# All eight PSUM banks as single ones of one pool, in both MLPs

## The chip, the core and the metric

The kernel runs on one core of a Trainium2 chip. The metric is the device time in microseconds (us) of one execution. Lower is better. The kernel runs three times, and the median is given beside a profile of one execution.

## What is computed

One inference step of a two-layer encoder on 576 frames (512 of a new stream, 64 of a running one) with 1024 features. Layer 0 mixes frames by causal pooling, layer 1 by sparse attention (an indexer scores the keys, the best are kept, softmax runs over these). Each is followed by an MLP with a squared ReLU:

```python
def _mlp(h, w_up, w_down):
    u = jax.nn.relu(h @ w_up)          # (frames, 1024) @ (1024, 4096)
    return (u * u) @ w_down            # (frames, 4096) @ (4096, 1024)

x = x + y                              # y from the pooling mixer or attention
x = x + _mlp(_rmsnorm(x, norm_mlp[i]), mlp_w_up[i], mlp_w_down[i])
```

A last RMS norm ends the step. The outputs are `y` for both streams, the new pooling states and the new keys, values and indexer keys.

## The kernel before

Everything stays on the core: `x`, the residual, is in SBUF as eight blocks of 128 features by 576 frames, and the weights stream through it. A float32 product is made of three matmuls: each operand is split into a high part (rounded to fp32r, a form that the matmul takes) and a low part that holds what was left. ACT makes the high part of a weight block (`wh`, L181), DVE the low part (`wl`, L182). Each matmul has a 128 x 128 weight and 288 frames (`HT`, half of 576), so one of its outputs fills 288 of the 512 float32 columns that a PSUM bank has.

PSUM has eight banks. A `stage` opens pools for a part of the program; `ps` is a pool of pairs (a tile of two neighbouring banks, taken with `psum`), `po` a pool of single banks (`psum1`). In the stages of both MLPs there are two pairs (banks 0 to 3) and four singles (4 to 7). Tiles of a pool are taken in the order in which its buffers come free.

An MLP has four chunks of 1024 hidden features. Chunk 0's Up part is a plain product: eight tiles (i = 0 to 7), each 48 matmuls by `project` (L305) into a tile `up` of two halves. `finished` then calls `activated`, which takes ReLU times the norm's factor (`rbm`, L460 or L462: one DVE instruction if the tile is a pair, two if it is a tuple of two singles) and squares it on ACT. All Up tiles are pairs but i = 2, which comes before the norm's factors are known.

All other parts use Strassen's scheme in the form with seven products. One "seven" (the function `seven`) makes a 2 x 2 block from seven products of twelve matmuls each (`product`, L504), in three single banks named `a`, `b` and `c`. Bank `b` takes b11, then t2, t3 and t4 in turn; between them the running sum is read out: after b11 ACT copies it to `a` (L533), and after t2, t3 and t4 the callbacks `b`, `hi1` and `lo1` read it. Bank `a` takes b21, bank `c` takes t1 and b22. So t4 may start only when the reading after t3 is done. The callbacks are in two classes: `Down` updates `x` on DVE (L562), `Up` reads the banks on DVE (L612 for `b` after t3, L618 for `c`, L595 for ReLU) and makes the operands of the Down products (`u`, with lower parts on DVE at L476). Chunks 1 to 3 have four Up sevens each, the last of them called final, and every chunk has four Down sevens, chunk 3 of layer 1 only three, since the last two output blocks are made as plain products at the end of the program (`last`, tiles `dn`). For these, `left_over` (L497) parks the hidden block b12 of each Up seven in PSUM, two to a pair, until the end.

The order of PE, DVE and ACT is made by a scheduler that plays the program forward with costs and sets each engine's instructions by when their operands and buffers come free; only in `last` is it written by hand. So the pools decide what stands between the products of a seven. Each engine then runs its list in order. A semaphore wait holds up all that stands behind it on that engine.

```python
    with stage(more=RAWS[1]):
        with stage(xs=1, slots=1, tmps=6, ps=3, po=2):
            pool_mixer()
        with stage(xs=1, u=1, acts=1, xt=1, sums=4, ps=2, po=4):
            mlp(0, 1, late=KT)
    with stage(under=1, xs=1, queries=1, slots=1, cst2=1, tmps=5), ExitStack() as parts:
        parts.enter_context(stage(ps=2, po=4))
        attention(parts)
    with stage(u=1, xs=1, acts=1, xt=1, sums=4, more=RAWS[1], ps=2, po=4):
        mlp(1, 3, end=last)
```

The attention stage has the same two pairs and four singles before and after. Its first work is the projections `pj` (L305), in pairs.

Of the kernel before, what the change touches and what calls it, by code (L numbers as in the profile page):

```python
# [12 lines left out]
ALU = mybir.AluOpType  # L13
# [3 lines left out]
P = 128  # L17
# [5 lines left out]
HT = T // 2  # L23
# [23 lines left out]
RAWS = (4, 3)  # L47
# [9 lines left out]
def pool_dsa_kernel(ctx: ExitStack, tc: tile.TileContext, a, o):  # L57
    nc = tc.nc
    act, dve, pool, pe = nc.scalar, nc.vector, nc.gpsimd, nc.tensor
# [11 lines left out]
    def uid(s):  # L71
        count[0] += 1
        return f"{s}_{count[0]}"
# [3 lines left out]
    @contextmanager  # L77
    def stage(**pools):


        with ExitStack() as st:
            for name, bufs in pools.items():
                space = {"space": PSUM} if name in ("ps", "po") else {}
                phase[name] = st.enter_context(tc.tile_pool(name=uid(name), bufs=bufs, reuse_waits="tile", **space))
                st.callback(phase.pop, name)
            yield
# [7 lines left out]
    def pair_slot(tag, s, dt=F32R, n=T):  # L94
        return slot(tag, s, dt)[:, :2 * n].rearrange("p (h t) -> p h t", h=2)
# [9 lines left out]
    def psum(s="ps"):  # L105
        return phase["ps"].tile([P, 2, 512], F32, tag="ps", name=uid(s))

    def psum1(s="po"):
        return phase["po"].tile([P, 512], F32, tag="po", name=uid(s))

    def f32(t):
        return t.bitcast(F32)

    def halves(t):
        return t.rearrange("p (h t) -> p h t", h=2)
# [165 lines left out]
    def next_block(sub=dve):  # L281
        return [next_unit(5 - i, sub) for i in range(2)]

    def at(w, k):

        return [t[:, (k % 4) * P:(k % 4 + 1) * P] for t in w[k // 4]]

    def split(dst, src, scale=None, sub=dve):

        if scale is None:  # L290
            act.copy(dst[:, 0], src)
            sub.tensor_tensor(dst[:, 1], src, f32(dst[:, 0]), ALU.subtract)
        else:
            act.activation(dst[:, 0], src, AF.Copy, scale=scale)
            dve.scalar_tensor_tensor(dst[:, 1], src, scale, f32(dst[:, 0]), ALU.mult, ALU.subtract)

    def project(pt, w, xs, between=iter(()), cols=((0, HT), (HT, HT))):

        n = len(xs)
        for k in range(n):  # L300
            next(between, None)
            wh, wl = at(w, k)
            for i, (wt, part) in enumerate(((wh, 0), (wh, 1), (wl, 0))):
                for h, (c, m) in enumerate(cols):
                    pe.matmul(  # L305
                        pt[h][:, :m] if isinstance(pt, tuple) else pt[:, h, :m], wt, xs[k][:, part, c:c + m],
                        start=(k == 0 and i == 0), stop=(k == n - 1 and i == 2),
                    )
# [76 lines left out]
    def split_x(gi, norm, room, late=0):  # L385

        xs = []
        for k in range(KT + late):
            if k < KT:
                t = room(k)  # L390
                split(t, x[k], gv[:, gi, k:k + 1])
                xs.append(t)
            if k >= late:
                norm.add(k - late)
        return xs

    def mlp(layer, gi, late=0, end=None):
# [13 lines left out]
        xs = split_x(gi, norm, lambda k: pair_slot("xs", "xs"), late)  # L411
# [4 lines left out]
        xt = []  # L416
        parked = []
# [74 lines left out]

        def left_over(j, b12):

            if j % 2 == 0:
                parked.append(psum("rest"))
            act.copy(parked[-1][:, j % 2, :HT], b12)  # L497

        def product(bank, w, operand, factor, js, first=False):
            for j in js:  # L500
# [175 lines left out]
        todo, us = [], []  # L676
        for i in range(KT):
            w = next_block()
            pt = (psum1("up"), psum1("up")) if i == 2 else psum("up")
            project(pt, w, xs, spread() if i == 2 else iter(()))  # L680
            todo.append((i, pt, us))
            if i == 1:
                norm.stats()
            if i < 2:
                continue
            for t in todo:
                finished(*t)
            todo.clear()
            if i in (3, 5):
                r = 2 * i - 6  # L690
                x_sums(i // 2 - 1, rough[:, r:r + 3], rough[:, r + 3])
# [17 lines left out]
        for c in range(1, 4):  # L709
            us = []  # L710
            for j in range(half):
                up = Up(c, j)
# [7 lines left out]
        if end:  # L720
            rest = []
            for j in range(half):
                if j % 2 == 0:
                    t = x_sums_tile()
                rest.append(t[:, j % 2])
                split(rest[j], parked[j // 2][:, j % 2, :HT])
            b11, b22, b21 = ([u[:, FACTORS.index(f)] for u in us] for f in ("b11", "b22", "b21"))
            end([rest + b22, b11 + b21])

    def last(parts):  # L730

        norm = Norm("f", lambda: slot("xs", "sq", F32)[:, :T])
        for k in range(KT - LAST):
            norm.add(k)
        ws = [next_block() for _ in range(LAST)]

        def finish(c, n, aside, rest):
            t = slice(c, c + n)
            room = halves(slot("xs", "room", F32))
            st = psum1("st")  # L740
            token_sums(st, norm.s2[:, t], n=n, block=BLOCK, final=False)
            if c:
                awake(KEEP[0])
            token_sums(st, rest, n=n, block=BLOCK, first=False)
            r = rms(st, n, BLOCK)
            if c:
                awake(KEEP[1])
            for k in aside:
                act.activation(x[k][:, t], x[k][:, t], AF.Copy, scale=gv[:, 4, k:k + 1])
            yield  # L750
            diag = diagonals(r, n, room[:, 0], BLOCK)
            banks = [psum1("rb") for _ in range(2 if c else 1)]
            for pb in banks:
                pe.matmul(pb[:, :n], ones[:BLOCK], diag[:BLOCK, :n], start=True, stop=True)
            pb = banks[0]
            rb = room[:, 1, :n]
            act.copy(rb, banks[-1][:, :n])
            yield
            for k in range(KT):
                if k == 4:  # L760
                    yield
                if k in aside:
                    pool.tensor_tensor(x[k][:, t], x[k][:, t], rb, ALU.mult)
                else:
                    dve.scalar_tensor_tensor(x[k][:, t], x[k][:, t], gv[:, 4, k:k + 1], pb[:, :n], ALU.mult, ALU.mult)
                if c and k > 3:
                    (nc.sync if k % 2 else act).dma_start(o["y"][:, k, t], x[k][:, t])
                elif k % 2:
                    nc.sync.dma_start(o["y"][:, k - 1:k + 1, t], x.t[k // 2][:, :, t])

        def awake(n):

            pt = psum("dn")
            for _ in range(n):
                pe.matmul(pt[:, 0, :HT], ws[0][0][0][:, :P], parts[0][0][:, 0], start=True, stop=True)

        def during(steps):

            for k in range(LAST * KT):
                if k in NORM_STEPS:  # L780
                    next(steps)
                yield

        before = between = iter(())
        with tc.manual_schedule(engines={ENG.PE, ENG.DVE, ENG.Activation}):
            for c, n, us in ((0, HT, parts[0]), (HT, HT, parts[1])):
                t = slice(c, c + n)
                s2 = norm.s2[:, t]
                for j in range(LAST):
                    k = KT - LAST + j  # L790
                    pt = psum("dn")
                    project(pt, ws[j], us, between, cols=((0, n),))
                    dve.tensor_tensor(x[k][:, t], x[k][:, t], pt[:, 0, :n], ALU.add)
                    sq = norm.room()[:, :n]
                    act.activation(sq, x[k][:, t], AF.Square)
                    if j < LAST - 1:
                        dve.tensor_tensor(s2, s2, sq, ALU.add)
                for _ in before:
                    pass
                before = finish(c, n, FINAL_ASIDE[c > 0], sq)  # L800
                between = during(before)
            for _ in before:
                pass
# [675 lines left out]
    x = Residual()  # L1479
    with stage(more=RAWS[1]):  # L1480
        with stage(xs=1, slots=1, tmps=6, ps=3, po=2):
            pool_mixer()
        with stage(xs=1, u=1, acts=1, xt=1, sums=4, ps=2, po=4):
            mlp(0, 1, late=KT)
    with stage(under=1, xs=1, queries=1, slots=1, cst2=1, tmps=5), ExitStack() as parts:
        parts.enter_context(stage(ps=2, po=4))
        attention(parts)
    with stage(u=1, xs=1, acts=1, xt=1, sums=4, more=RAWS[1], ps=2, po=4):
        mlp(1, 3, end=last)


# [94 lines left out]
```

## Time and profile before

| | |
|---|---|
| median of 3 runs | 1085.96 us (1085.89 to 1086.33) |
| profiled execution | 1085.9 us, its span 1084.1 us |
| PE (matmul) busy | 1051.9 us, 97% of the span |
| DVE busy | 909.1 us, 84% |
| ACT busy | 627.1 us, 58% |
| POOL busy | 264.6 us, 24% |
| layer 0's MLP | about 41 to 414 us |
| attention | about 414 to 690 us |
| layer 1's MLP and the end | about 690 to 1084 us |

PE is TensorE's matmul queue, PEld its weight loads, DVE the vector engine, ACT the scalar engine, POOL GpSimd. In a row of a timeline stand the start (us), the duration, the engine, the line, the operation, the output and its inputs, and their shapes; several of the same kind in a row are one row with their count, and the bracket names the idle time ahead of it and what ended that. A row of waits gives the total, the times and the longest. In windows each engine has its busy time and a count of instructions; behind POOL stand the granted PE clock, the DMA share and GB/s.

### The profile page before, as it was taken

The page shows a single profiled execution, that of the slowest core. Times are in us where ns is not written, and L with a number is a line of the kernel's source. Part 1 is how long each engine was busy: PE and PEld are TensorE (multiplying, and loading weights), DVE is VectorE, ACT ScalarE, POOL GpSimd, SP SyncE. Part 2 cuts the span into 40 slices and gives each one's busy share as a digit, 9 for nine tenths or more (in the row PEclk, how much of TensorE's full clock was granted, in tenths as well). Part 3 has the DMA queues.
Part 4 walks back from the last instruction along what each step waited for, and adds up shares of the span by engine and source line. Part 5 has one row for each costly group of instructions (what it writes and reads, how often), then busy time and mean ns, then how long its engine had stood idle before and what let it go on. Part 6 is the DMA issues. An engine that isn't in the chain of part 4 may idle for free.

```text
span 1084.1 us, 21647 instructions
## 1 busy us (share of the span) xinstructions
PE 1051.9 (97%) x7942; PEld 1024.0 (94%) x7942; DVE 909.1 (84%) x1845; ACT 627.1 (58%) x1240; POOL 264.6 (24%) x285
## 2 busy tenths in 40 slices
PE   9999999999999999999999999999999999999996
PEld 8999998999999999999988888999999999999895
DVE  7788989879978987869999944688989879979974
ACT  8555466447546654444477776455467447547641
POOL 4100111111111100237686892000111111111001
PEclk9999999999999999999989999999999999999998
DMA  8343676676676654447632454333676666667512
GB/s 252 94 102 89 171 166 151 166 163 169 151 166 165 156 161 165 128 153 191 201 108 68 129 170 123 126 108 97 166 165 157 162 164 165 154 170 161 125 51 88
DMA packets 94459, 157.66 MB, mean 145 GB/s; under 512 B 13729, under 2 KB 25296, under 8 KB 94352
## 3 DMA queue, kind: packets, MB, share of 16 engines
q1 hardware_dynamic: 68720, 109.80, 33.3%
q0 software_dynamic: 15840, 28.84, 17.1%
q10 hardware_dynamic: 9792, 17.63, 5.2%
q8 instruction: 62, 1.02, 0.4%
q14 instruction: 45, 0.37, 0.1%
HBM read 141.15 MB, written 10.89 MB: 140 GB/s over the span
## 4 chain that ended last, share of the span: by engine, by line
PE 78%; DVE 9%; ACT 3%; POOL 3%; issue 3%; DMA 2%; SPq 0%; DVEq 0%; POOLq 0%; ACTq 0%
PE b L504 28%; PE c L504 15%; PE up L305 9%; PE a L504 7%; PE pj L305 7%; PE wo L305 2%; DVE wl L182 2%; PE wa L305 1%; PE pb L1011 1%; PE sc L1284 1%; PE dn L305 1%; PE pt L1310 1%; POOL p L1263 1%; DVE u L476 1%; PE o L1342 1%
## 5 line engine op out<-in xcount | busy, mean ns | idle before, releaser
L181 ACT CAST wh<-raw 128x512 fp32r<-128x512 f32 (+1 forms) x316 | 194.8, 620 | 232.6 <-PE b L504 75.4
L182 DVE TENSOR_TENSOR wl<-raw,wh 128x512 fp32r<-128x512 f32 (+1 forms) x294 | 205.9, 703 | 38.6 <-ACT wh L181 30.2
L504 PE MATMUL b<-u,wh 128*128 128x288 f32 x992 | 203.1, 296 | 2.2 <-ACT a L533 1.7
L504 PEld LDWEIGHTS b<-u,wh 128*128 128x128 f32 x992 | 159.5, 188 | 4.3 <-ACT a L533 3.6
L181 ACT CAST wh<-sum 128x512 fp32r<-128x512 f32 x165 | 101.4, 620 | 80.3 <-PE b L504 36.3
L504 PE MATMUL b<-u,wl 128*128 128x288 f32 x496 | 145.5, 296 | 0.0
L182 DVE TENSOR_TENSOR wl<-sum,wh 128x512 fp32r<-128x512 f32 x165 | 112.0, 687 | 20.6 <-ACT wh L181 18.5
L238 POOL DMA_DIRECT2D sum<-in_w_down x31 | 27.1, 891 | 327.4 <-DVE u L476 86.6
L504 PE MATMUL c<-u,wh 128*128 128x288 f32 x496 | 103.3, 297 | 0.9 <-DVE u L476 0.6
L504 PEld LDWEIGHTS b<-u,wl 128*128 128x128 f32 x496 | 92.8, 188 | 0.0
L305 PE MATMUL up<-xs,wh 128*128 128x288 f32 x512 | 89.6, 296 | 1.0 <-DVE x L1477 0.8
L504 PE MATMUL b<-xt,wh 128*128 128x288 f32 x384 | 77.9, 296 | 8.0 <-DVE v L612 8.0
L476 DVE TENSOR_TENSOR u<-v,u 128x864 fp32r<-128x864 f32 (+2 forms) x100 | 82.1, 825 | 0.9 <-ACT u L473 0.5
L504 PEld LDWEIGHTS c<-u,wh 128*128 128x128 f32 x496 | 80.1, 188 | 2.5 <-DVE x L562 1.5
L473 ACT CAST u<-v 128x864 fp32r<-128x864 f32 (+2 forms) x100 | 72.7, 730 | 8.8 <-DVE v L491 5.4
L504 PE MATMUL b<-xs,wh 128*128 128x288 f32 x384 | 76.8, 295 | 0.0
L305 PEld LDWEIGHTS up<-xs,wh 128*128 128x128 f32 x512 | 74.6, 188 | 2.0 <-ACT wh L181 1.0
L504 PE MATMUL c<-u,wl 128*128 128x288 f32 x248 | 73.2, 295 | 0.0
L238 POOL DMA_DIRECT2D sum<-in_w_up x24 | 20.7, 863 | 209.4 <-DVE wl L182 132.5
L504 PEld LDWEIGHTS b<-xt,wh 128*128 128x128 f32 x384 | 61.3, 188 | 9.6 <-DVE v L612 9.6
L454 ACT ACTIVATE v<-v 128x288 f32<-128x288 f32 (+1 forms) x112 | 52.0, 476 | 16.5 <-DVE v L595 14.1
L305 PE MATMUL pj<-xs,wh 128*128 128x288 f32 x352 | 61.3, 295 | 0.0
(287 smaller groups left out, 2738.4 us busy)
## 6 DMA issues: line engine op xcount, KB each, us to landing
raw<-in_w_up SPq DMA_DIRECT2D x128, 256.0 KB, 3.0
raw<-in_w_down SPq DMA_DIRECT2D x128, 256.0 KB, 2.9
raw<-in_w_o ACTq DMA_DIRECT2D x32, 256.0 KB, 2.8
sum<-in_w_down SPq DMA_DIRECT2D x31, 256.0 KB, 2.9
sum<-in_w_down POOLq DMA_DIRECT2D x31, 256.0 KB, 4.5
raw<-in_w_down POOLq DMA_DIRECT2D x31, 256.0 KB, 5.0
raw<-in_w_in ACTq DMA_DIRECT2D x30, 256.0 KB, 3.0
sum<-in_w_up SPq DMA_DIRECT2D x24, 256.0 KB, 3.0
```

The lines of the kernel that those rows point to most:

```text
L181: act.copy(h, src)
L182: how["sub"].tensor_tensor(l, src, f32(h), ALU.subtract)
L238: pool.dma_start(s1, odd[:, 512:], accum_op=ALU.add)
L305: pe.matmul(pt[h][:, :m] if isinstance(pt, tuple) else pt[:, h, :m], wt, xs[k][:, part, c:c + m], start=(k == 0 and i == 0), stop=(k == n ...
L454: act.activation(v, v, AF.Square)
L473: act.copy(u[:, f, 0], v[:, f])
L476: dve.tensor_tensor(u[:, f, 1], v[:, f], f32(u[:, f, 0]), ALU.subtract)
L504: pe.matmul(bank[:, :HT], wt, ut, start=first and j == 0 and i == 0, stop=j == 3 and i == 2, skip_group_check=True)
L1011: pe.matmul(pt[:, c0:c0 + rhs.shape[1]], lhs, rhs, start=n == 0, stop=n == len(steps) - 1)
L1263: pool.tensor_scalar(p, p, rs[:, h:h + 1], 1.0, ALU.mult, ALU.mult)
L1284: pe.matmul(pt[:, hh, :nw], q[:, 2 * s + hh], ks[g][:, part, :nw], start=part == 0, stop=part == 1)
L1310: pe.transpose(pp[:, c:c + P], pr[:, hh, kt * P:(kt + 1) * P], ident)
```

## The change

Both MLP stages open one pool of eight single banks (`po=8`) and no pairs. What was in pairs moves to singles: the Up tiles of chunk 0, of which now all eight are tuples of two, the parked blocks b12, one bank each, and the tiles `dn` of the end.

```diff
         def left_over(j, b12):
-            if j % 2 == 0:
-                parked.append(psum("rest"))
-            act.copy(parked[-1][:, j % 2, :HT], b12)
+            parked.append(psum1("rest"))
+            act.copy(parked[-1][:, :HT], b12)
...
-            pt = (psum1("up"), psum1("up")) if i == 2 else psum("up")
+            pt = psum1("up"), psum1("up")
...
-                split(rest[j], parked[j // 2][:, j % 2, :HT])
+                split(rest[j], parked[j][:, :HT])
...
-            pt = psum("dn")
+            pt = psum1("dn")
...
-                    pt = psum("dn")
-                    project(pt, ws[j], us, between, cols=((0, n),))
-                    dve.tensor_tensor(x[k][:, t], x[k][:, t], pt[:, 0, :n], ALU.add)
+                    pt = psum1("dn")
+                    project((pt,), ws[j], us, between, cols=((0, n),))
+                    dve.tensor_tensor(x[k][:, t], x[k][:, t], pt[:, :n], ALU.add)
...
-        with stage(xs=1, u=1, acts=1, xt=1, sums=4, ps=2, po=4):
+        with stage(xs=1, u=1, acts=1, xt=1, sums=4, po=8):
             mlp(0, 1, late=KT)
...
-    with stage(u=1, xs=1, acts=1, xt=1, sums=4, more=RAWS[1], ps=2, po=4):
+    with stage(u=1, xs=1, acts=1, xt=1, sums=4, more=RAWS[1], po=8):
         mlp(1, 3, end=last)
```

The lines below L496 stand one lower after the change: L504 becomes L503, L562 becomes L561, L612 becomes L611. PE has 7678 matmuls in both programs, DVE 1781 instructions before and 1795 after; the counts of ACT, POOL and of the DMAs are the same.

DVE, the first Up tiles of chunk 0, `up`, that are read into `v` (i = 0 and 1 together, once the norm's factors `rbm` are there). Before:

```order
L182 TENSOR_TENSOR wl_911<-raw_395,wh_910 128x512
L462 SCALAR_TENSOR_TENSOR v_891<-up_687,rbm_149_866 128x2x288
L462 SCALAR_TENSOR_TENSOR v_891<-up_748,rbm_149_866 128x576
L182 TENSOR_TENSOR wl_917<-raw_401,wh_916 128x512
L484 TENSOR_TENSOR v_891<-v_891 128x288
L487 SCALAR_TENSOR_TENSOR v_891<-v_891 128x288
```

After:

```order
L182 TENSOR_TENSOR wl_912<-raw_395,wh_911 128x512
L460 SCALAR_TENSOR_TENSOR v_890<-up_684,rbm_150_865 128x288
L460 SCALAR_TENSOR_TENSOR v_890<-up_746,rbm_150_865 128x288
L460 SCALAR_TENSOR_TENSOR v_890<-up_685,rbm_150_865 128x288
L460 SCALAR_TENSOR_TENSOR v_890<-up_747,rbm_150_865 128x288
L182 TENSOR_TENSOR wl_918<-raw_401,wh_917 128x512
L484 TENSOR_TENSOR v_890<-v_890 128x288
```

Each L462 on 576 columns is two L460 on 288, and what follows keeps its place.

PE, where layer 0's MLP ends and attention begins. `b_5231` (before) and `b_5242` (after) are the bank `b` of the last Down seven, `pj` is attention's first projection. Before, the two rows that end t3 and what follows; t4, whose weights are `wh_5281` and `wl_5282`, comes after three more rows:

```order
L504 MATMUL b_5231<-u_4673,wh_5247 128x288 x2
L504 MATMUL b_5231<-u_4673,wl_5248 128x288
L305 MATMUL pj_5448<-xs_5394,wh_5298 128x288 x4
L305 MATMUL pj_5525<-xs_5394,wh_5336 128x288 x4
L305 MATMUL pj_5448<-xs_5394,wl_5299 128x288 x2
L305 MATMUL pj_5448<-xs_5394,wh_5298 128x288 x4
L305 MATMUL pj_5448<-xs_5394,wl_5299 128x288 x2
L305 MATMUL pj_5448<-xs_5403,wh_5298 128x288 x4
L305 MATMUL pj_5448<-xs_5403,wl_5299 128x288 x2
L305 MATMUL pj_5448<-xs_5403,wh_5298 128x288 x4
L305 MATMUL pj_5448<-xs_5403,wl_5299 128x288 x2
L305 MATMUL pj_5448<-xs_5414,wh_5317 128x288 x4
```

After, the two rows that end t3, then t4 (weights `wh_5292` and `wl_5293`), then `pj`:

```order
L503 MATMUL b_5242<-u_4684,wh_5258 128x288 x2
L503 MATMUL b_5242<-u_4684,wl_5259 128x288
L503 MATMUL b_5242<-u_4219,wh_5292 128x288 x2
L503 MATMUL b_5242<-u_4219,wl_5293 128x288
L503 MATMUL b_5242<-u_4374,wh_5292 128x288 x2
L503 MATMUL b_5242<-u_4374,wl_5293 128x288
L503 MATMUL b_5242<-u_4529,wh_5292 128x288 x2
L503 MATMUL b_5242<-u_4529,wl_5293 128x288
L503 MATMUL b_5242<-u_4684,wh_5292 128x288 x2
L503 MATMUL b_5242<-u_4684,wl_5293 128x288
L305 MATMUL pj_5458<-xs_5404,wh_5309 128x288 x4
L305 MATMUL pj_5458<-xs_5404,wl_5310 128x288 x2
```

40 matmuls of `pj` stood between t3 and t4 and stand behind t4 now. The first `pj` pair is banks 0 and 1 now as before; bank 0 is now the `c` of this seven. On DVE the updates (L562, now L561), weight splits and norm steps around it stand in the same order as before.

PE, layer 1, chunk 3, the second Up seven. `b_12885` (before) and `b_12906` (after) are its bank `b`, `b_13041` and `b_13063` that of the third seven, `c_13043` its bank `c`. Before, the two rows that end t3 and what follows; t4, whose weights are `wh_12937` and `wl_12938`, comes after six more rows:

```order
L504 MATMUL b_12885<-xs_9154,wh_12901 128x288 x2
L504 MATMUL b_12885<-xs_9154,wl_12902 128x288
L504 MATMUL b_13041<-xs_9139,wl_12961 128x288
L504 MATMUL b_13041<-xs_9143,wh_12960 128x288 x2
L504 MATMUL b_13041<-xs_9143,wl_12961 128x288
L504 MATMUL b_13041<-xs_9149,wh_12960 128x288 x2
L504 MATMUL b_13041<-xs_9149,wl_12961 128x288
L504 MATMUL b_13041<-xs_9154,wh_12960 128x288 x2
L504 MATMUL b_13041<-xs_9154,wl_12961 128x288
L504 MATMUL c_13043<-xt_9501,wh_12981 128x288 x2
L504 MATMUL c_13043<-xt_9501,wl_12982 128x288
```

After, the two rows that end t3, then t4 (weights `wh_12958` and `wl_12959`), then the third seven:

```order
L503 MATMUL b_12906<-xs_9161,wh_12922 128x288 x2
L503 MATMUL b_12906<-xs_9161,wl_12923 128x288
L503 MATMUL b_12906<-xt_9514,wh_12958 128x288 x2
L503 MATMUL b_12906<-xt_9514,wl_12959 128x288
L503 MATMUL b_12906<-xt_9665,wh_12958 128x288 x2
L503 MATMUL b_12906<-xt_9665,wl_12959 128x288
L503 MATMUL b_12906<-xt_9960,wh_12958 128x288 x2
L503 MATMUL b_12906<-xt_9960,wl_12959 128x288
L503 MATMUL b_12906<-xt_10106,wh_12958 128x288 x2
L503 MATMUL b_12906<-xt_10106,wl_12959 128x288
L503 MATMUL b_13063<-xs_9146,wh_12981 128x288 x2
L503 MATMUL b_13063<-xs_9146,wl_12982 128x288
```

22 matmuls of the third seven stood between t3 and t4 and stand behind t4 now. At the final Up seven of layer 0's chunks 2 and 3 and of layer 1's chunk 2 it is the other way: no matmul stood between t3 and t4, and now 16 do, taken from the matmuls around, while t4 keeps its number among PE's matmuls from the program's start.

More of the change, by code (lines that the diff above doesn't have):

```diff
@@ L771, in awake @@
         def awake(n):
-            pt = psum("dn")
+            pt = psum1("dn")
             for _ in range(n):
-                pe.matmul(pt[:, 0, :HT], ws[0][0][0][:, :P], parts[0][0][:, 0], start=True, stop=True)
+                pe.matmul(pt[:, :HT], ws[0][0][0][:, :P], parts[0][0][:, 0], start=True, stop=True)
         def during(steps):
```

## The prediction

> **What bounds the kernel now.** I read the page from the top: first the busy time of each engine, then the chain of work that ended last, then the waits of PE, then busy time by stage, and last the timelines of the places where the change moves something.
>
> ```profile
> span 1084.1 us, 21647 instructions
> PE 1051.9 (97%) x7942; PEld 1024.0 (94%) x7942; DVE 909.1 (84%) x1845; ACT 627.1 (58%) x1240; POOL 264.6 (24%) x285
> PE 78%; DVE 9%; ACT 3%; POOL 3%; issue 3%; DMA 2%; SPq 0%; DVEq 0%; POOLq 0%; ACTq 0%
> ```
>
> PE is busy for 97% of the span and holds 78% of the chain. A change that leaves the number of matmuls alone, as this one does, can only win or lose in the 32.2 us (1084.1 less 1051.9) in which PE is not busy. The profiled execution took 1085.9 us, its span 1084.1, so 1.8 us lie around the span. It stands 0.06 us under the median of the three runs, 1085.96, and the sum below starts from 1085.9.
>
> Next, PE's waits that belong to the two MLPs (total us, times, longest):
>
> ```profile
> PE b L504 <- DVE v L612: 8.0, 7, 1.3
> PE b L504 <- ACT a L533: 1.7, 5, 1.0
> PE c L504 <- DVE u L476: 0.6, 1, 0.6
> ```
>
> The first is the large one: bank `b` is read by DVE (L612, the reading of t3's bank by `hi1`) and PE, which wants to start t4 into the same bank, waits. It happens seven times for 8.0 us. The question is whether more banks take it away. The windows say no. They list, for a stretch, its length and then the busy time of PE, PEld, DVE, ACT and POOL:
>
> ```profile
> 41.00:103.00 62.00, 61.74 (x462) 60.85 (x462) 51.17 (x89) 34.25 (x57) 3.46 (x5) 1.00 0.34 86
> 270.00:280.00 10.00, 8.89 (x67) 8.66 (x66) 10.00 (x21) 6.66 (x14) 1.72 (x2) 1.00 0.64 139
> 360.00:370.00 10.00, 8.87 (x67) 8.64 (x66) 10.00 (x19) 7.32 (x15) 1.75 (x2) 1.00 0.70 157
> 410.00:419.00 9.00, 9.00 (x70) 9.00 (x69) 9.00 (x16) 4.96 (x9) 0.00 (x0) 1.00 0.47 160
> 414.00:480.00 66.00, 65.14 (x497) 64.28 (x496) 45.76 (x82) 29.46 (x56) 10.34 (x6) 1.00 0.53 161
> 480.00:600.00 120.00, 115.31 (x866) 109.04 (x865) 115.00 (x334) 70.12 (x186) 89.96 (x79) 0.96 0.48 133
> 996.00:1016.00 20.00, 19.99 (x152) 19.75 (x151) 19.39 (x37) 15.08 (x32) 3.45 (x4) 1.00 0.72 169
> ```
>
> Around the stalls at 278 and 369 DVE is busy for 10.00 of 10.00 us, PE for 8.9. So at the end of a chunk's Up part DVE is the bound; PE is ahead and waits for a backlog.
>
> **The final Up products, where the wait is: nothing.** One stall, PE and then DVE:
>
> ```profile
> 276.96 0.29 PE L504 MATMUL b<-xs,wl 128*128 128x288 f32 x1
> 278.37 0.53 PE L504 MATMUL b<-xt,wh 128*128 128x288 f32 x2 [1.11 <-DVE v L612]
> 277.50 0.45 DVE L618 TENSOR_TENSOR v<-c,snap 128x288 f32<-128x288 f32 x1
> 277.87 0.45 DVE L612 TENSOR_TENSOR v<-b,snap 128x288 f32<-128x288 f32 x1
> ```
>
> PE could issue the next matmul about 0.13 us after 276.96 (the step between matmuls: 1.22 us for eight in the `pj` row below, 0.29 for one); it issues at 278.37, 0.05 after DVE's read ends at 277.87 + 0.45. In the new order 16 matmuls of other banks stand between t3 and t4 of this seven where none stood before. But they were taken from behind and in front of it: t4 is the same matmul by number from the program's start, and DVE's read of the bank comes behind the same work, plus seven instructions from the block products early in the MLP. DVE at 10.00 of 10.00 can't come earlier, so t4 can't either. I take 0, with ±1.0 over all seven stalls for what the order of weight splits does to single ones (a single L182 takes a step of 0.60, below).
>
> The Trainium skill has a rule that speaks the other way: Perfetto Trace Analysis, section Optimization Strategy, says that the same gap repeating on the engine that should be saturated can mean too little SBUF or PSUM for the next tile. By that rule the seven gaps are a want of banks and the 8.0 us would go. The rows with DVE at 10.00 of 10.00 are why I weigh it as a rival and not as the forecast.
>
> **Up tiles as two singles: fourteen more DVE instructions.** Seven of eight Up tiles of each MLP become tuples, and `activated` runs two L460 on 288 columns in place of one L462 on 576. Both stand in the trace, two of each back to back:
>
> ```profile
> 61.76 1.43 DVE L462 SCALAR_TENSOR_TENSOR v<-up,rbm 128x576 f32<-128x576 f32 x2 [2.26 <-ACT rbm L336]
> 68.55 0.81 DVE L460 SCALAR_TENSOR_TENSOR v<-up,rbm 128x288 f32<-128x288 f32 x2
> 62.06 0.42 PE L305 MATMUL up<-xs,wl 128*128 128x288 f32 x2
> 62.57 0.40 PE L305 MATMUL up<-xs,wh 128*128 128x288 f32 x1
> ```
>
> Two L460 end after 0.81 us; one L462 takes half of 1.43 and a little, 0.75 with its tail. So each costs about 0.07 us more, 1.0 us for 14. Cover: the window 41:103 has DVE busy 51.17 of 62.00, so most is hidden; the ends are 0 and +1.0, and I take +0.2, being nearest to the hidden end. Against it stands a small gain: PE stops at 62.06 + 0.26 and goes on at 62.57, since the tile i = 3 takes a pair that DVE's first L462 must release. With eight singles that tile finds banks that only ACT's copies of `rb` hold. That gives up to 0.25 us, and 0.5 if layer 1 is alike. I take −0.5 and so −0.3 for this part (ends −0.5 and +0.5).
>
> **Entry into attention: a new stall.** This is the largest term. The last Down seven of layer 0 and what PE and DVE do around it:
>
> ```profile
> 413.87 0.29 PE L504 MATMUL b<-u,wl 128*128 128x288 f32 x1
> 414.00 1.22 PE L305 MATMUL pj<-xs,wh 128*128 128x288 f32 x8
> 419.28 0.42 PE L504 MATMUL b<-u,wh 128*128 128x288 f32 x2
> 414.12 0.45 DVE L562 TENSOR_TENSOR x<-x,c 128x288 f32<-128x288 f32 x1
> 414.48 1.29 DVE L182 TENSOR_TENSOR wl<-raw,wh 128x512 fp32r<-128x512 f32 x2
> 415.69 0.45 DVE L562 TENSOR_TENSOR x<-x,b 128x288 f32<-128x288 f32 x1
> 421.07 0.45 DVE L562 TENSOR_TENSOR x<-x,b 128x288 f32<-128x288 f32 x1 [1.66 <-PE b L504]
> ```
>
> Before, t3 ends with the row at 413.87, and PE fills the time until DVE has read `b` (415.69 + 0.45) with 40 matmuls of attention's projection `pj`, which sits in the pairs that the sevens don't touch. Only at 419.28 comes t4. After, all banks belong to the MLP's turn; `pj`'s first tile takes in the bank of this same seven's `c`, and the order has t4 directly behind t3, with `pj` behind it. DVE's order there is the same, row for row, and the window 410:419 has it busy 9.00 of 9.00, so its read still ends at 416.14. PE then stands from 414.00 to 416.19: 2.2 us. If DVE had come there earlier and only the read itself stayed between t3 and t4, 0.5 us would be left (0.45 + 0.05); that is the lower end. Behind the waiting t4 on PE's queue are all of the 40 `pj` matmuls, and ACT and DVE wait for those (rotary, then the index scores). Payback: in 414:480 PE lost only 66.00 − 65.14 = 0.86 us, so no more than 0.86 is to be had there; in 480:600 DVE is at 115.00 of 120.00 and could absorb some, but its work starts from `pj`, which is late. What does come earlier is the last update of `x` (421.07 before) and the norm's sums behind it. I take 0.6 back, from the 0.86: +1.6, ends −0.4 (0.5 − 0.86) and +2.2.
>
> **Layer 1, chunk 3, second Up seven: a new stall, half of it repaid.** Before, 22 matmuls of the next seven stood between t3 and t4; after, none:
>
> ```profile
> 993.22 0.43 PE L504 MATMUL b<-xs,wl 128*128 128x288 f32 x2
> 996.27 0.42 PE L504 MATMUL b<-xt,wh 128*128 128x288 f32 x2
> 993.25 0.68 DVE L264 TENSOR_TENSOR sum<-sum,raw 128x512 f32<-128x512 f32 x1
> 993.85 0.45 DVE L612 TENSOR_TENSOR v<-b,snap 128x288 f32<-128x288 f32 x1
> 994.22 0.45 DVE L595 SCALAR_TENSOR_TENSOR v<-v,rbm 128x288 f32<-128x288 f32 x1
> 1018.03 0.54 PE L504 MATMUL b<-xt,wh 128*128 128x288 f32 x2 [1.12 <-DVE v L612]
> ```
>
> The row at 993.22 holds the last matmul of t3 and the first of the next seven, so PE is free at about 993.36. DVE's read of `b` begins at 993.85; after the change one L595 more stands ahead of it (a step of 0.37, from 993.85 to 994.22), so it ends at 994.67 and t4 begins at 994.72: 1.36 us lost. But DVE is nearly full there (19.39 of 20.00 in 996:1016), so PE only comes to a later stall with less lead: the final Up's wait of 1.12 at 1018.03 can shrink by as much as was lost. Ends: 0 and +1.4, and −0.3 if the reads come in a better order. I take the middle, +0.6. That each of the four parked b12 has a bank of its own changes no count: four copies (L497) before and after, and none of them was waited for.
>
> **What is the same.** The order of the last Down sevens and of the end (`last`) is unchanged, so `dn` in a single costs nothing. In attention behind `pj` a few dozen matmuls and DVE steps trade places where PE, DVE and POOL all wait by turns; 0 ± 1.0, from PE's 120.00 − 115.31 = 4.7 us of waiting in 480:600, of which the order moves a small part.
>
> **Sum.** 0 − 0.3 + 1.6 + 0.6 + 0 = +1.9 on 1085.9: 1087.8 us. 0.2% of it (2.2 us, so 1083.8 and 1088.1) is about what a measurement of this kernel can tell from no change.
>
> **The rivals.**
>
> Faster: a shortage of banks did cause the L612 waits, since free banks let PE and DVE drift further apart over a whole chunk and DVE's backlog at its end is shorter. All 8.0 gone, with the rest of the sum, gives 1079.8; half gives 1083.8, so it decides from half on. For it: it is seven times the same wait on a bank. Against: DVE at 10.00 of 10.00, and no DVE work is taken away. I see some 1082 if it holds.
>
> Slower: both new stalls stay whole (2.2 and 1.4) and the longer pairs of L460 are on the path (1.0): 4.6, 1090.5. For it: PE is at 99% in 414:480, with little to give back. Against: DVE's slack in 41:103, and the repayment in a stretch that DVE bounds.
>
> Nothing: PE's stall at the entry is made up where DVE and POOL bound attention, and the rest cancels: 1085 to 1086.4.
>
> **Chances.** Forecast (1086.4 to 1088.9) 0.45, faster 0.20, slower (above 1088.9) 0.20, nothing 0.15. Of the forecast's own range some four tenths lie above 1088.1, so slower by over 0.2% has 0.20 + 0.17 = 0.37, same 0.15 + 0.28 = 0.43, faster 0.20. The range leaves a tenth out on each side: 1082.0, the faster case's likely figure, to 1090.6, the slower case's own.
>
> **What would show it.** Right: a PE wait of about 2 us on DVE's L561 read (the new number of L562) between t3 and t4 where attention begins; the seven waits on L611 still 7 to 8 us in total, with one more of 1.0 to 1.4 in layer 1's chunk 3; 32 L460 in place of 4, and no L462. Wrong: L611's waits fall below 4 us, or the stall at the entry is missing, or PE's busy time in attention shows it repaid before 600 us.

## The result: 0.8% slower, five times the loss that was forecast

| | before | after |
|---|---|---|
| median | 1085.97 us (4 runs, 1085.89 to 1086.33) | 1095.58 us (4 runs, 1092.42 to 1096.29) |
| profiled execution | 1085.9 us | 1095.71 us, its span 1093.9 us |

The ratio after to before is 1.008, with a 95% interval of 1.0064 to 1.0095. The runs after spread over 3.9 us, those before over 0.4.

The page of the changed kernel, its totals, and then PE's waits in the MLPs:

```profile
span 1093.9 us, 21604 instructions
PE 1054.4 (96%) x7942; PEld 1027.8 (94%) x7942; DVE 911.0 (83%) x1859; ACT 629.9 (58%) x1240; POOL 264.6 (24%) x285
```

```profile
PE b L503 <- DVE v L611: 14.2, 7, 2.6
PE b L503 <- DVE x L561: 2.1, 1, 2.1
```

DVE has 1.9 us more work (911.0 against 909.1), PE waits 14.2 us in place of 8.0 for the same kind of read, and 2.1 us for the new one at the entry. The count is seven in both, but not the same seven. Before, five were at final Up sevens and two (1.32 and 1.33 us) at the third Up seven of chunk 1 in either layer. After, these two are gone, six are at the final Up sevens (1.82 to 2.55 us), and one of 1.83 is the new one in chunk 3 of layer 1. PE's busy time also grew, by 2.5 us, though it runs the same matmuls. In three stretches there the clock was lower. Windows of the changed kernel (length; busy time of PE, PEld, DVE, ACT and POOL with their counts; PEclk; DMA share; GB/s) just behind three of the waits:

```profile
187.50:190.90 3.40, 3.40 (x15) 3.40 (x16) 3.24 (x10) 2.22 (x6) 0.00 (x0) 0.50 0.12 41
419.60:423.00 3.40, 3.40 (x16) 3.40 (x15) 2.94 (x6) 0.84 (x2) 0.00 (x0) 0.50 0.49 159
1003.30:1006.70 3.40, 3.40 (x17) 3.40 (x16) 3.14 (x7) 2.69 (x5) 0.00 (x0) 0.50 0.35 113
```

The granted clock is 0.50, and the windows hold 15 to 17 matmuls in 3.40 us, where one at the full clock holds 28 (below, at the busy entry). The records of the clock give such a stretch 3.41 us. At the half clock matmuls start 0.24 us apart and otherwise 0.132, so a stretch sets PE back by up to 3.41 x (1 - 0.132/0.24) = 1.5 us, on top of the wait ahead of it; less where PE would have waited again soon after. In attention the changed kernel has one such stretch fewer than before (6.83 us of half clock against 10.24).

Both kernels run the same number of matmuls, so the two traces can be laid side by side by number: how much later the matmul of the same number starts after the change. Three such pairs (the index scores' first product in attention, the first Up product of layer 1, the last norm), PE's timeline of before and then of after:

```profile
468.50 0.39 PE L1204 MATMUL ix<-kis,qi 128*128 128x256 f32 x1 [0.21 <-DVE wi L1188]
689.77 0.37 PE L305 MATMUL up<-xs,wh 128*128 128x288 f32 x1 [0.77 <-DVE x L1477]
1066.81 0.51 PE L754 MATMUL rb<-room,ones 96*128 96x288 f32 x1 [0.69 <-DVE room L345]
```

```profile
475.39 0.38 PE L1203 MATMUL ix<-kis,qi 128*128 128x256 f32 x1 [0.15 <-DVE wi L1187]
696.02 0.37 PE L305 MATMUL up<-xs,wh 128*128 128x288 f32 x1 [0.78 <-DVE x L1476]
1076.60 0.51 PE L753 MATMUL rb<-room,ones 96*128 96x288 f32 x1 [0.69 <-DVE room L345]
```

They are 6.89, 6.25 and 9.79 us apart. The same for every hundredth matmul gives this account of one profiled execution each:

| stretch | later at its end | added |
|---|---|---|
| start of the program, ahead of the MLP | 1.26 | +1.26 |
| layer 0, Up tiles of chunk 0 | 0.74 | -0.5 |
| layer 0, the three final Up sevens and what follows them | 3.10 | +2.4 |
| entry into attention | 6.97 | +3.9 |
| attention | 6.27 | -0.7 |
| layer 1, Up tiles | 5.57 | -0.7 |
| layer 1, chunks 1 and 2 | 7.05 | +1.5 |
| layer 1, chunk 3 and the end | 9.78 | +2.7 |

The first line isn't the change's: that part of the program is the same, and in the traces below it lies between 0.0 and +1.3 at its end; why wasn't looked into.

The entry, the changed kernel's timeline, PE and DVE:

```profile
416.89 0.30 PE L503 MATMUL b<-u,wl 128*128 128x288 f32 x1
419.30 0.54 PE L503 MATMUL b<-u,wh 128*128 128x288 f32 x2 [2.12 <-DVE x L561]
419.64 0.44 PE L503 MATMUL b<-u,wl 128*128 128x288 f32 x1
419.88 0.68 PE L503 MATMUL b<-u,wh 128*128 128x288 f32 x2
422.04 1.15 PE L305 MATMUL pj<-xs,wh 128*128 128x288 f32 x4
418.71 0.45 DVE L561 TENSOR_TENSOR x<-x,b 128x288 f32<-128x288 f32 x1
```

t3 ends, PE stands idle for 2.12 us until DVE has read `b`, and then the clock falls: a pair of matmuls that took 0.43 takes 0.68, four of `pj` take 1.15 where they took 0.69.

### The profile page after: what moved, and what is told of

It is laid out like the page before. It is cut to its first block, busy times and chain, and to the rows that moved or that the text cites. A ratio compares the mean times of both kernels' runs of the same rounds, so it can differ in the third digit from the quotient of the medians.

```text
span 1093.9 us, 21604 instructions
## 1 busy us (share of the span) xinstructions
PE 1054.4 (96%) x7942; PEld 1027.8 (94%) x7942; DVE 911.0 (83%) x1859; ACT 629.9 (58%) x1240; POOL 264.6 (24%) x285
## 4 chain that ended last, share of the span: by engine, by line
PE 48%; DVE 7%; DMA 2%; issue 2%; POOL 2%; ACT 1%; SPq 0%; DVEq 0%; POOLq 0%; ACTq 0%
PE b L503 15%; PE c L503 7%; PE pj L305 6%; PE up L305 5%; PE a L503 3%; PE wo L305 2%; PE sc L1283 2%; PE wa L305 2%; DVE wl L182 2%; PE pt L1309 1%; DMA raw<-in_w_in 1%; PE dn L305 1%; PE o L1334 1%; PE o L1341 1%; DVE u L476 1%
## 5 line engine op out<-in xcount | busy, mean ns | idle before, releaser
L503 PE MATMUL b<-u,wh 128*128 128x288 f32 x992 | 203.2, 297 | 2.2 <-DVE x L561 2.1
L503 PEld LDWEIGHTS b<-u,wh 128*128 128x128 f32 x992 | 160.2, 190 | 3.4 <-ACT sq L322 2.3
L503 PE MATMUL b<-u,wl 128*128 128x288 f32 x496 | 146.0, 297 | 0.0
L503 PE MATMUL c<-u,wh 128*128 128x288 f32 x496 | 102.7, 296 | 1.4 <-DVE u L476 0.7
L503 PEld LDWEIGHTS b<-u,wl 128*128 128x128 f32 x496 | 93.3, 189 | 0.0
L503 PE MATMUL b<-xt,wh 128*128 128x288 f32 x384 | 79.5, 300 | 14.2 <-DVE v L611 14.2
L503 PEld LDWEIGHTS c<-u,wh 128*128 128x128 f32 x496 | 80.0, 189 | 2.6 <-DVE u L476 1.2
L473 ACT CAST u<-v 128x864 fp32r<-128x864 f32 (+2 forms) x100 | 72.6, 730 | 11.1 <-DVE v L491 9.4
L503 PE MATMUL b<-xs,wh 128*128 128x288 f32 x384 | 78.0, 297 | 0.0
L503 PEld LDWEIGHTS b<-xt,wh 128*128 128x128 f32 x384 | 62.3, 191 | 15.9 <-DVE v L611 15.9
L503 PE MATMUL c<-u,wl 128*128 128x288 f32 x248 | 73.2, 295 | 0.0
L503 PEld LDWEIGHTS b<-xs,wh 128*128 128x128 f32 x384 | 62.1, 191 | 0.0
```

Source lines behind the costliest of these rows:

```text
L473: act.copy(u[:, f, 0], v[:, f])
L503: pe.matmul(bank[:, :HT], wt, ut, start=first and j == 0 and i == 0, stop=j == 3 and i == 2, skip_group_check=True)
```

## The experiments

Each was timed beside the kernel before, on the same chip. Theory A, after the result: the time is lost by the order that eight shared banks give the sevens and the entry, with the half clock behind the longer waits.

**Two pools of four.** The Up tiles, the parked blocks and `dn` have four singles of their own (taken with `psumu`), the sevens the other four.

```diff
-        with stage(xs=1, u=1, acts=1, xt=1, sums=4, po=8):
+        with stage(xs=1, u=1, acts=1, xt=1, sums=4, pu=4, po=4):
...
-            pt = psum1("up"), psum1("up")
+            pt = psumu("up"), psumu("up")
```

> Both MLPs have eight singles, but in two pools of four: the sevens draw on banks 4 to 7 alone, as before the change, and the Up tiles, the parked blocks and dn on four singles of their own in place of the two pairs. So the Up tiles are tuples and DVE has the 14 more L460, while the sevens and the entry into attention stand in the order of before. Theory A (the time was lost by the order that eight shared banks give the sevens and the entry): 1084.5 to 1086.5 us, before's time less up to 1 us for the wait at the Up tiles that goes. Rival B (the tuples themselves, the longer DVE work in L460 or the start of the program, cost it): 1090 to 1096.

Measured: 1092.88 us (5 runs, 1091.75 to 1094.97), ratio 1.0058 [1.0045, 1.0071]. Theory A's number was missed and rival B's range was hit, but not by rival B's cause, and the trace says why. In the sevens and at the entry nothing was lost: it is 3.4 us behind before at matmul 800 and 2.7 at matmul 3100, past the entry. The loss is at the first Up tiles of both layers (1.3 to 4.7 in layer 0, 2.0 to 6.0 in layer 1):

```profile
58.40 1.24 PE L338 MATMUL rb<-xt,ones 128*128 128x288 f32 x4 [2.17 <-DVE xt L348]
708.12 1.21 PE L338 MATMUL rb<-xt,ones 128*128 128x288 f32 x4 [2.26 <-DVE xt L348]
```

Tiles i = 0 and 1 hold all four banks until the norm's factors are there, so tile i = 2 can't fill the time in which the norm is worked out. This was a fault of the experiment, mended below.

**Layer 0 alone, layer 1 alone.** The stages of one MLP have `po=8`, the other's `ps=2, po=4`.

> Only layer 0's MLP has the eight singles of one pool; layer 1's has two pairs and four singles as before. Theory A: what the changed kernel's trace had lost where attention ends (6.3 us, of them 4.0 at the entry into attention), so 1089.5 to 1092.5. Rival C (the loss is in layer 1, and what stood at 6.3 is a matter of that one execution): 1086 to 1088.

> Only layer 1's MLP has the eight singles of one pool. Theory A: the 3.5 us that the changed kernel's trace lost behind attention, nearly all in chunk 3, so 1088.5 to 1090.5. Rival C: 1093 or more. If the two layers add up, the losses of this and of the kernel with layer 0 alone sum to that of the changed kernel, 9.6.

Measured: 1090.93 us (1089.62 to 1093.41), ratio 1.0042 [1.0029, 1.0054], and 1091.15 us (1089.67 to 1091.76), ratio 1.0036 [1.0022, 1.005]; before beside them 1086.28 (9 runs, 1084.68 to 1087.78). Both layers lose, 4.7 and 4.9 us, and the two add up to 9.5, the changed kernel's loss being 9.6 (by the ratios 0.42 and 0.36%, against 0.8%). Layer 1's is above the range expected, 1088.5 to 1090.5: in that trace 1.5 us fell in attention, whose program is unchanged. In layer 0's trace the entry cost 4.0 us (3.27 later at matmul 3000, 7.26 at 3100), with a half clock of 3.41 us from 421.0 on.

**No parking.** The b12 blocks aren't copied away.

```diff
-            parked.append(psum1("rest"))
-            act.copy(parked[-1][:, :HT], b12)
+            parked.append(b12)
...
-                split(rest[j], parked[j][:, :HT])
+                split(rest[j], norm.rb[:, :HT])
```

> The changed kernel without the copies that park the four blocks b12: nothing is parked, and the last product takes other data in their place (so y's last features are left out of what it computes). Chunk 3 of layer 1 then has all eight banks, and the order of its sevens becomes that of chunks 1 and 2: 31 and 16 matmuls between t3 and t4 of the last two Up sevens in place of 12 and 0. Theory A with the parking as cause of chunk 3's loss: the stall of 2.0 us at its second Up seven goes with the half clock behind it, 2.5 to 4 us less than the changed kernel beside it, 1091.5 to 1093.5. Rival D (parking plays no part, chunk 3 loses by DVE's backlog alone): 1095 to 1096.

Measured: 1094.42 us (5 runs, 1092.43 to 1095.22), ratio 1.0069 [1.0056, 1.0081], above theory A's range and below rival D's. In chunk 3 the trace goes from 7.98 us behind before at matmul 7300 to 8.51 at the end, where the changed kernel goes from 7.06 to 9.78. So the four parked singles do make most of chunk 3's loss; its second Up seven has no wait of 1 us or more, and the final one waits 1.87 us as in the other chunks. The loss against the kernel before beside it is 8.1 us, only 1.5 less than the changed kernel's 9.6: this execution had half clocks in other places (at 373.6, behind a final Up, and at 479.4), and the runs' spread of 2.8 us is wider than the effect. Here the trace decides, one execution of each, and not the total. Its entry has the wait of 2.1 us without a half clock behind it, and cost 2.4 us.

**Two pools of four, tile i = 2 from the sevens' four**, the first experiment mended:

```diff
-            pt = psumu("up"), psumu("up")
+            pt = (psum1("up"), psum1("up")) if i == 2 else (psumu("up"), psumu("up"))
```

> As the kernel with two pools of four singles, but the Up tile i = 2 takes its two banks from the sevens' pool, as before the change; in the first kernel all three first Up tiles shared four banks, and its trace lost 3.4 us in layer 0 and 4.0 us in layer 1 just there, and nothing in the sevens or at the entry. Theory A (tuples cost nothing, only the order of the sevens and of the entry does): with that loss gone, 1084.5 to 1087 us, same as before beside it; at matmul 500 of layer 0 it is no more than 0.3 us behind before, from the start of the MLP on. Rival B (the tuples cost by themselves): 1088 or more.

Measured: 1087.12 us (12 runs, 1086.14 to 1088.0), before 1086.34 (29 runs, 1084.16 to 1089.36), ratio 1.0007 [0.9998, 1.0015]. No difference that can be told, 0.1 us above the range named, and its trace ends 0.6 us behind before. Its waits on the read of `b`, and its entry:

```profile
PE b L506 <- DVE v L614: 7.2, 6, 1.3
```

```profile
413.67 0.30 PE L308 MATMUL pj<-xs,wh 128*128 128x288 f32 x1
418.96 0.43 PE L506 MATMUL b<-u,wh 128*128 128x288 f32 x2
```

All pairs are singles here, the 14 more L460 are in it, and `pj` again fills the time between t3 and t4 (413.67 to 418.96). The tuples cost nothing that can be told, 1.6 us at most by the interval. What costs is that the sevens, the parked blocks and attention's first tiles take turns in one set of eight.

**A busy entry.** Layer 0 alone, with matmuls that nobody reads where PE stood idle.

```diff
+                if factor == "t4" and getattr(on, "close", False):
+                    hot = psum1("hot")
+                    for _ in range(16):
+                        pe.matmul(hot[:, :HT], w[0][:, :P], operand(3, "t3", 0), ...)
```

> Layer 0 alone changed, with 16 more matmuls into a bank that nobody reads, placed between the third and fourth products of bank b of the last Down seven of layer 0 (15 of them stand between t3 and t4, with four of c, where PE stood idle for 2.1 us). They are 2.1 us of work and save no wait. If the half clock of 3.4 us behind that wait is a second loss beside the wait itself (theory E: the wait costs 2.3, the slow stretch 1.6), PE stays busy and the clock full: the trace's loss from matmul 3000 to 3100 falls from 4.0 to 2.3 to 2.9 us, and the time is 0.5 to 2 us less than that of layer 0 alone (1090.93): 1089 to 1090.5. Rival F (the slow stretch has nothing to do with the wait): the clock halves as before, and the 16 matmuls come on top or change nothing: 1091 to 1093.

Measured: 1089.75 us (12 runs, 1087.86 to 1090.4), ratio 1.0027 [1.0018, 1.0036], 1.2 us less than layer 0 alone, though it has 16 matmuls more; the two intervals overlap, so the total alone doesn't show the gain. The window behind its entry, and then the one behind the entry's wait with layer 0 alone:

```profile
419.60:423.00 3.40, 3.40 (x28) 3.40 (x27) 3.40 (x7) 3.19 (x6) 0.00 (x0) 1.00 0.66 208
```

```profile
421.00:424.40 3.40, 3.40 (x17) 3.40 (x16) 3.16 (x6) 1.97 (x3) 0.00 (x0) 0.50 0.71 262
```

With PE kept busy the clock stays at 1.00, and the window holds 28 matmuls, not 17. The loss around the entry is 2.1 us, the time of the 16 matmuls themselves, counted from matmul 2900 (3.66 to 5.75, since five of the sixteen stand ahead of t3), against 3.9. The other traces with this entry say the same without added matmuls: from matmul 3000 to 3100 the three with a half clock behind the wait lost 4.0 us (the changed kernel, layer 0 alone, less DVE work), the two without it 2.4 (no parking, and the changed kernel with splits on POOL). At the entry the half clock is a loss of its own, 1.5 us, and follows from the idle time.

**Less DVE work.** In `Up.hi0`, for the changed kernel and for the one before:

```diff
-                first_sum(v)
-                middle_sums(v)
+                act.copy(v[:, 2], v[:, 4])
+                act.copy(v[:, 3], v[:, 5])
```

> The changed kernel with less DVE work in the Up sevens: the three sums behind the reading of bank c (L484, L487 and L488) are left out and two copies on ACT stand for them, so y is not what is asked for. 16 sevens of layer 0 and 12 less... in all 24 Up sevens, 1.1 us of DVE work each. If DVE's backlog is what PE waits for at the final Up sevens (theory G), the seven waits on L611 shrink from 14.2 us to under 6 in all, each to under 1 us. Rival H (the waits come from the banks or from latency): they stay above 10 us. The entry's wait on L561 stays near 2 us under both, since DVE's work there is not touched.

> The same work left out of the kernel before. Theory G: the waits on L612, 8.0 us in seven, fall under 3 us, and the time to 1078 to 1083 us. What is left between this kernel and the changed one with the same work left out is what eight shared banks cost where DVE isn't the bound: theory G says the entry (4 us) and chunk 3 of layer 1, 3 to 6 us in all; if the banks helped once DVE is not the bound, the changed one would be level or faster.

Measured: 1086.45 us (10 runs, 1084.4 to 1087.56) for the changed kernel, 1082.38 (4 runs, 1081.97 to 1082.52; ratio 0.996 [0.9945, 0.9976]) for before. The waits on the read of `b`, first of the changed kernel, then of before:

```profile
PE b L503 <- DVE v L611: 7.8, 7, 1.9
PE b L503 <- DVE x L561: 2.1, 1, 2.1
```

```profile
PE b L504 <- ACT u L473: 4.6, 5, 0.9
PE b L504 <- ACT a L533: 3.3, 7, 0.6
PE b L504 <- DVE v L612: 1.2, 1, 1.2
```

With DVE relieved, before keeps 1.2 of its 8.0 us on that read: the waits at the final Up sevens were DVE's backlog. In their place PE now waits for ACT, which has taken over two copies per seven: 3.3 us on L533 where it was 1.7, and 4.6 on L473 (five times 0.9, behind the final Up sevens). So the 4.0 us by which the time fell aren't the 6.8 us of waits that went; in the trace 2.3 fell in the two MLPs and 1.9 in attention, which had one half-clock stretch in place of three. The changed kernel keeps 7.8 of 14.2 (more than the 6 expected): five of 0.8, and two in chunk 3 of layer 1, 1.90 and 1.87. The two medians are 4.1 us apart, and the changed kernel with less DVE work only comes level with the whole kernel before (ratio 0.9997).

The two relieved kernels, laid side by side by number, show where eight shared banks lose and where they win: the changed one comes out of the entry 3.9 us later than it went in, and of chunk 3 and the end 2.5 us later (3.7 at matmul 7400, with a half clock). But it gains 1.8 us in the rest of layer 0's MLP and 1.3 in layer 1's Up tiles and chunks 1 and 2. So where DVE isn't the bound, more banks are worth some 3 us (one trace each), and the two places cost more than that.

**A weight split on POOL**, 24 of them, as a kernel that might beat both: `ahead(sub=pool)` in `Up.lo0`.

> The kernel before, with one of the seven low parts of a weight block (L182) in each of the 24 Up sevens made on POOL in place of DVE: 0.6 us less for DVE per seven, 1.3 us of work for POOL, which is idle there but for its DMAs. Nothing is left out. Theory G (DVE's backlog makes the waits at the final Up sevens): the waits on L612, 8.0 us, fall to under 3 us and the time to 1080 to 1084 us. Rival I (POOL's slower split, or its DMAs that now stand behind it, take the gain): 1085 or more.

> The same move of 24 splits to POOL in the changed kernel. Theory G: the waits on L611 at the final Up sevens fall below 1.5 us each, so few of them have a half clock behind them, but the entry into attention (2.1 us) and chunk 3's second Up seven keep theirs: 1085 to 1090 us, 3 to 6 us more than the kernel before with the same move. If eight shared banks were worth something once DVE is relieved, the two would be level.

Measured: 1104.73 us (4 runs, 1101.34 to 1107.55), ratio 1.0167 [1.0148, 1.0186], and 1107.55 us (5 runs, 1105.34 to 1108.33), ratio 1.0192 [1.0178, 1.0206]. A miss for both; of the rivals, I holds. While POOL splits, DVE's own instruction beside it stretches (timeline of the first of the two):

```profile
155.93 1.31 POOL L182 TENSOR_TENSOR wl<-raw,wh 128x512 fp32r<-128x512 f32 x1 [7.10 <-ACT wh L181]
156.02 1.54 DVE L488 TENSOR_TENSOR v<-v 128x288 f32<-128x288 f32 x1
```

L488 takes 0.45 us in the kernel before. DVE's busy time grew (926.5 us against 909.1) although 24 instructions left it. In that trace 37 DVE instructions took over 0.2 us more than the median of their kind before, 27 of them beside a split on POOL, and these 27 make 33.7 of the 39.9 us so added. That it is POOL's split that holds them up is argued from this, not tested apart.

## Why the prediction was wrong, point by point

- **Direction and the two new places: right.** Slower, by a new wait at the entry and one in chunk 3, with the Up tiles a little faster (-0.3 forecast, -0.5 and -0.7 measured).
- **The entry: the wait right, its price wrong.** 2.2 us was forecast and 2.1 measured, and L561 stands at 418.71, exactly where 415.69 and the 3.02 us by which the kernel was late there put it. The step that failed is the payback of 0.6 and what follows the wait: at matmul 3100 nothing had come back, and the half clock had added 1.5. The term was +1.6 and measured +3.9. By the end of attention 0.7 had come back, but attention also had one half-clock stretch fewer, so this doesn't show a payback.
- **The final Up sevens: the term of 0 was the largest error.** It measured +3.9 (2.4 in layer 0, 1.5 in chunks 1 and 2 of layer 1). The bound was right (DVE's backlog; the runs with less DVE work show it), and so was that more banks don't remove the waits, though two of the seven did go, which were not at final sevens. But the step that put t4 where it was, since DVE's read "comes behind the same work", failed: in the new order other work stands ahead of the read. The waits of the final sevens in the other chunks grew by 0.7 us each; in chunk 1 one of 2.55 and one of 2.52 stand for 2.22 (two waits) and 1.33. In chunk 2 of layer 0, from one read of `b` to the next, before and after:

```profile
266.11 0.45 DVE L612 TENSOR_TENSOR v<-b,snap 128x288 f32<-128x288 f32 x1
277.87 0.45 DVE L612 TENSOR_TENSOR v<-b,snap 128x288 f32<-128x288 f32 x1
```

```profile
267.64 0.45 DVE L611 TENSOR_TENSOR v<-b,snap 128x288 f32<-128x288 f32 x1
279.84 0.45 DVE L611 TENSOR_TENSOR v<-b,snap 128x288 f32<-128x288 f32 x1
278.22 0.29 PE L503 MATMUL b<-u,wl 128*128 128x288 f32 x1
280.34 0.53 PE L503 MATMUL b<-xt,wh 128*128 128x288 f32 x2 [1.82 <-DVE v L611]
```

  DVE needs 12.20 us where it needed 11.76: in the new order one more weight split (a step of 0.60) stands ahead of the read and one reading of bank `c` (L617, 0.37) behind it, and the remaining 0.2 us are short gaps between its instructions. PE reached t4 0.7 us earlier relative to DVE's read, of these 0.44 from DVE and the rest from small losses of PE that went. In the two traces with two pools of four that stretch is 11.74 and 11.72. Chunk 2 also lost 1.4 us more behind t4, where the next Down seven asked for the final `u` sooner; chunk 3 did not. By matmul number chunk 1 of layer 0 cost 0.5 us, chunk 2 1.8 and chunk 3 nothing.
- **Chunk 3 of layer 1: +0.6 forecast, +2.7 measured.** The extra L594 (0.37) ahead of the read was seen rightly. But DVE itself came 0.6 us later there relative to PE, so the wait, counted as the prediction counts it, was 1.99 us and not 1.36 (1.83 in the profile's count). The step "half of it repaid" failed: the final Up's wait did not shrink but grew, from 1.12 to 1.83, since t4 stands nine matmuls, 1.2 us, earlier in PE's order. And one half clock came on top, 1.5 us where it fell.
- **The rivals.** The slower rival (1090.5) had both new waits whole, which was right, but no place for the longer waits at the final Up sevens or for the clock. The faster one is refuted for this kernel: the gaps repeat, but they follow DVE's work, and with twice the banks for the sevens their total rose from 8.0 to 12.4 us, without the new one in chunk 3. The Trainium skill (Perfetto Trace Analysis, Optimization Strategy) says only that such consistent bubbles can mean too little SBUF or PSUM for the next tile, and here they did not.
- **Left out altogether: the half clock.** Three stretches lie in the MLPs and at the entry, but they don't cost 1.5 us each. At the entry it is 1.5. Behind the final Up seven of chunk 1 in layer 0 it is 0.3: traces without that stretch ("no parking", "a busy entry") have two more waits there instead, 1.1 us together. In chunk 3 it is 1.5 where it fell (3.6 us lost from matmul 7300 to 7400, against 2.1 with the same wait and no stretch there, in layer 1 alone); some 0.9 us of the whole came back by the end. So the clock makes, as an estimate from these, 1.8 to 3.3 of the 9.8 us. Its sign was in the profile of before, a PEclk of 0.96 in 480:600, and was read as a matter of attention alone.

Attention's own differences go largely with the clock too. The kernel before has three stretches there, the changed one two. Of the twelve traces the three with one stretch come out of attention 1.2 to 3.2 us less behind than they went in, the five with two 0.6 to 1.8 less, the two others with three 1.3 and 1.5 more, the one with four 1.2 more. What stays open: chunk 3's loss with the parked blocks and no half clock at all, which no trace shows, and how many stretches the runs without a trace had.

## What to carry to other kernels

Before giving more banks to one pool, look at what stands between a bank's last read and the next write of it, and at who takes over the banks when the stage ends: here a pair that the old stage had left free let the next stage's matmuls cover a wait, and sharing it uncovered the wait. Where an engine is full, compare the time of the work ahead of a read in the two orders, not the count. And price a wait of PE with what the clock does behind it, and with whether PE would have waited again just there.

## What the runs showed of the hardware

Whether a wait of PE brings the half clock can be read from these traces. In each of the twelve, all records of the clock begin on one grid of 3.413 us, which lies differently against the program in every execution (the first record begins 4.4 to 7.3 us into the span). What counts is PE's idle time within one window of the grid, and the clock of the next window follows from it. The entry on the grid, first the changed kernel, then the kernel without parking:

```profile
416.21:419.63 3.42, 1.30 (x10) 1.10 (x9) 3.42 (x7) 1.86 (x3) 0.00 (x0) 1.00 0.47 153
419.63:423.04 3.41, 3.41 (x17) 3.41 (x16) 2.95 (x6) 0.88 (x2) 0.00 (x0) 0.50 0.51 160
```

```profile
417.97:421.38 3.41, 1.62 (x12) 1.65 (x13) 3.41 (x7) 1.86 (x3) 0.00 (x0) 1.00 0.73 229
421.38:424.79 3.41, 3.41 (x28) 3.41 (x27) 3.17 (x6) 2.24 (x4) 0.00 (x0) 1.00 0.72 251
```

The wait is 2.1 us in both. In the first it lies in one window, which so is idle for 2.12 of 3.41 us. In the second a border cuts 0.32 us off, 1.79 are left, and the clock stays. Over the twelve traces, outside attention (its entry is in) and the program's first 41 and last 40 us, 2572 windows ran at the full clock: of the 19 with 1.80 us or more of idle time all 19 were followed by the half clock, of the 8 with 1.70 to 1.80 two, and of the 2545 with less one. Of the changed kernel's eight waits of 1.8 us or more, three lie in one window whole and have the half clock behind them; the other five are cut by a border, to 1.66 us or less in either window, and have none. Before, all waits in the MLPs are 1.33 us or less, and no half clock lies there. So the same wait costs more or less by where the grid lies, which the program doesn't set. That fits the wider spread of the changed kernel's first runs (3.9 us against 0.4), but isn't its only source: beside the experiments the kernel before spread as well, over 1084.2 to 1089.4 us.

The Trainium skill (TensorE: Matmul & The Clock Gate, section Part 1: The HAM clock gate) states a free-running window of 3413 ns, and that the clock falls to half rate after an idle window; the grid and the length of a stretch agree with it. The rule of no idle gaps above some 3.4 us, which the Trainium skill gives on the same page (section HAM oscillation), isn't enough in these traces: some waits of 1.72 us and more were followed by the half clock.

And a DVE instruction (L488) that takes 0.45 us took 1.54 us beside a split of 1.31 us on POOL.
